# In one pair of attention tiles, Q and K change places in the seven-product scheme, and K's second half is put out last

## The chip, the cores and the metric

The kernel runs on one core of a Trainium2 chip. The metric is the device time of one execution in microseconds. Three executions of the kernel before took 2127.22, 2127.66 and 2129.57 us; the median, 2127.66 us, is the time before.

## The reference

The model is a decoder trunk of two layers over 1024 positions of width 1024. Layer 0 mixes tokens with a spatial gate, layer 1 with dilated attention; each is followed by a dense MLP. The change lies in the attention layer, which computes, cut to what matters:

```python
qkv = (h @ w_qkv).astype(float32).reshape(B, S, 3, 3, 8, 64)      # Q, K, V; 3 dilation groups; 8 heads
for g, (window, dil) in enumerate(((128, 1), (512, 4), (2048, 16))):
    # blocks of 128 queries against their own and the previous block of keys, keys gathered by stride
    s = einsum('bnqrhc,bnkrhc->bnrhqk', q, k) * 64 ** -0.5
    logits = where(valid, s + bias, -1e30)
    m = max(logits); p = exp(logits - m); den = sum(p); num = einsum('bnrhqk,bnkrhc->bnqrhc', p, v)
# the three groups' numerators and denominators are merged per head with exp(m_g - max m)
o = num_sum / den_sum
return o @ w_out
```

## The kernel before, in words

**Units.** The attention is cut into 12 units: four pairs of heads, and for each the three dilation groups in the order 1, 2, 0. A unit has three tiles of 128 columns of `w_qkv`: tile 0 is Q, tile 1 is K, tile 2 is V. A tile (i, m) is tile m of unit i. Unit 1 is group 2 of the first pair of heads, unit 2 is group 0 of the same heads.

**Pairs.** After a start by plain products, the tiles are computed two at a time, in the order of the list `quads` (L1568 to L1570). Two tiles, the two halves of the contraction and the two halves of the sequence make a 2x2 block product, done by `seven` (L1224) with seven block products in the place of eight. One block product is 12 matmuls of 128x512 on the tensor engine: four slices of the contraction, three matmuls each, because every fp32 operand is split in a high and a low part. The products come in the order 6, 1, 5, 7, 2, 3, 4. The four results are ready at different times: result (1, 1), the second tile's second half of the sequence, after product 7; (0, 0) after product 2; (0, 1) after product 3; (1, 0) after product 4. The first index is the tile's place in the pair. In the pair that the change touches, number 1 in the list, K of unit 2 had place 0 and Q of unit 2 place 1.

**Putting a result out.** `put_out` calls `out_qk` (L1190) for Q and K: an addition on the vector engine (L1205), where the result is a sum of two, then the high part on the scalar engine (L1209) and the low part on the vector engine (L1210). Where the first half of a K is put out, the tile's slots are taken, and the recording of the program first goes on with the attention until the scores of the unit before are all recorded (`flow.until(lambda: U[i - 1].scored.t is not None)`, L1195). Only the tensor engine's order is kept as it is recorded; a scheduler orders the other engines.

**Attention beside the products.** `attention` (L1351) is a generator that `flow.pump()` resumes between the products' matmuls, at times that the program estimates with fixed latencies. For each unit and each of four blocks j it issues the transposes of the probabilities (`turned`, L1313: L187 in the profile, `at<-ident,t`), the scores of the next block (`scores`, L1288: `at<-k,q`), and the products of probabilities and V (`values`, L1326: `at<-tr,V`). Behind the scores stand the vector engine's reductions (L1307) and four exponentials on the scalar engine (L1309); behind the transposes a split in high and low part (`tr`, L205 on the scalar engine, L206 on the vector engine); behind the values two copies to `N` (L1346). In the profile the products of a pair read `mm<-y,wp` or `mm<-t,wp`, by the kind of their moving operand.

**Other work around it.** Each pair's weights are loaded by the sync engine's queue (`r<-in_w_qkv`), combined on GpSimd and split on the scalar and vector engines while the pair before runs. When unit 0's values are done, its `N` is stored to memory (`away<-N`, L1391), and K of unit 2 takes the slot that this `N` held. When a unit's scores are done, its statistics go out and come back in another order (`sc<-st`, `ex<-sc`, L1432 and L1434), for the merge of the groups (L1450 on).

Of the kernel before, what the change touches and what calls it, by code (L numbers as in the profile page):

```python
# [33 lines left out]
def blk(b, n=1):  # L34
    return slice(b * P, (b + n) * P)
# [77 lines left out]
def trunk(ctx: ExitStack, tc: tile.TileContext, xT, w_u, w_v, w_o, w_s, b_s, w_qkv, w_bo, rel,  # L113
          w_up, w_dn, w_dl, vecs, onehot, outT):
    nc = tc.nc
    flow = Flow()
# [56 lines left out]
    def mm_bank():  # L173
        return psm.tile([P, HALF], F32, tag="mm", name="mm")
# [33 lines left out]
    def weight(src, place=None):  # L208
        place = place or (lambda name: wpool.tile([P, D], F32R, tag="w", name=name))
        lo, hi = place("wlo"), place("whi")  # L210
        for i in range(2):
            split(hi[:, half(i)], lo[:, half(i)], load(src[:, half(i)]))
        return hi, lo
# [215 lines left out]
    def plain(src):  # L429
        w = {}  # L430
        for j in range(2):
            for i in range(2):
                w[i, j] = wpair().split(load(src(i, j)))
        return w

    def up(layer, q):
        return lambda i, j: w_up[layer, q, i, j]
# [86 lines left out]
    def load_x(s, k):  # L524
        i = nc.sync.dma_start(h[k][:, half(s)], xT[k * P:(k + 1) * P, half(s)])
        if s:
            tc.keep_in_program_order(i)
        return i
# [100 lines left out]
    for gi, chunks in enumerate(((0, 1, 2), (3, 4, 5), (6, 7))):  # L629
        banks = {}  # L630
        for k in range(KT):
            if gi == 0:
                x = load_x(0, k)
                scaled(0, k)
            if gi == 0 or gi == 1 and k > 1:
                with tc.issue_after((gelus[5] if gi else x).ins):
                    w = weight(w_v[k])
            else:
                w = weight(w_v[k])
# [20 lines left out]
            for e, i, n, f in order:  # L660
                x, c = ys[n // 4][k], blk(n % 4)
# [30 lines left out]
    for tiles in ((0, 1, 2), (3,), (4,), (5, 6, 7)):  # L692
        w = [weight(w_u[m]) for m in tiles]
        for s in range(2):
            for i, m in enumerate(tiles):
                b = mm_bank()
# [9 lines left out]
    for tiles in ((0, 1), (2,), (3,), (4, 5, 6, 7)):  # L706
        w = [weight(w_o[m]) for m in tiles]
        for s in range(2):
            for i, m in enumerate(tiles):
                b = mm_bank()  # L710
# [3 lines left out]
            if tiles[-1] == 7:  # L714
                start_terms(sq[s], s, 1, terms)
                if s == 0:
                    first = [plain(up(0, q)) for q in range(2)]
# [324 lines left out]
    xa = Terms()  # L1042
# [45 lines left out]
    def order_of(two):  # L1088

        a, b = (U[i].g for i, _ in two)  # L1090
        return b if a == b or 0 in (a, b) else 0
# [65 lines left out]
    def out_v(i, s, a, b, go):  # L1157

        u = U[i]
        ready = []  # L1160
        with tc.high_priority(offset=PRIO):
            if u.g < 2:
                t = temp()
                if b is None:
                    put(stored(t, u.g), runs(a, u.g), None)
                elif go == u.g:
                    put(stored(t, go), stored(a, go), runs(b, go))
                elif u.g == 0:
                    put(unrolled(t, go), a.rearrange("p (r q) -> p q r", r=DIL[go]), unrolled(b, go))
                else:  # L1170
                    put(t.rearrange("p (r q) -> p q r", r=4), own(a, u.g), own(b, u.g))
                ready.append((s, t))
            else:
                for e in range(2):
                    if e not in u.vt:
                        u.vt[e] = temp()
                    c = slice(8 * e, 8 * e + 8)
                    if b is None or go == 2:
                        put(u.vt[e].rearrange("p (r q) -> p r q", r=8)[:, :, 32 * s:32 * s + 32],
                            (runs if b is None else stored)(a, 2)[:, c, :], None if b is None else runs(b, 2)[:, c, :])  # L1180
                    else:
                        put(u.vt[e].rearrange("p (r q) -> p q r", r=8)[:, 32 * s:32 * s + 32, :], own(a, 2)[:, :, c],
                            own(b, 2)[:, :, c])
                u.out += 1
                if u.out == 2:
                    ready = [(e, u.vt.pop(e)) for e in range(2)]
        for part, t in ready:
            flow.add(v_side(i, t, part), LAT["ve"] + (500 if b is None else 1500) + (5000 if i == 0 else 0))

    def out_qk(i, m, s, a, b, over, go):  # L1190

        u = U[i]
        if m not in u.tiles:
            if m == 1 and i > 0:
                flow.until(lambda: U[i - 1].scored.t is not None)  # L1195
            u.tiles[m] = [slot((P, S), F32R, f"{'qk'[m]}{e}") for e in range(2)]
        hi, lo = (runs_at(t, s, u.g) for t in u.tiles[m])
        sc = -0.125 if m == 0 else 1.0
        with tc.high_priority(offset=PRIO):
            if b is None:  # L1200
                a = stored(a, go) if over else runs(a, u.g)
            else:
                t = a if over and u.g == go else temp()
                if u.g == go:
                    nc.vector.tensor_tensor(stored(t, go), stored(a, go), runs(b, go), op=ALU.add)  # L1205
                else:
                    nc.vector.tensor_tensor(t.rearrange("p (r q) -> p q r", r=DIL[u.g]), own(a, u.g), own(b, u.g), op=ALU.add)
                a = stored(t, u.g)
            nc.scalar.activation(hi, a, AF.Copy, scale=sc)  # L1209
            nc.vector.scalar_tensor_tensor(lo, a, sc, hi.bitcast(F32), op0=ALU.mult, op1=ALU.subtract)  # L1210
        u.out_qk = getattr(u, "out_qk", 0) + 1
        if u.out_qk == 4:
            u.q, u.k = u.tiles[0], u.tiles[1]
            u.qk.t = flow.t

    def out(tile, s, a, b=None, over=False, go=0):

        i, m = tile
        if m == 2:
            out_v(i, s, a, b, go)  # L1220
        else:
            out_qk(i, m, s, a, b, over, go)

    def seven(w, x, more, put_out, begun=None, first=False, go=0):  # L1224

        def one(p, bank=None):
            new = bank is None
            bank = mm_bank() if new else bank
            product(bank, w[p], x.t[p], p in (2, 3, 4) and not (first and p == 3))
            more()  # L1230
            return bank

        def copied(src):
            t = temp()
            with tc.high_priority(offset=PRIO):
                nc.scalar.activation(stored(t, go), runs(src, go), AF.Copy)  # L1236
            return t

        def plus(x, y, out=None):
            out = temp() if out is None else out  # L1240
            with tc.high_priority(offset=PRIO):
                nc.vector.tensor_tensor(stored(out, go), stored(x, go), runs(y, go), op=ALU.add)
            return out

        if first:
            a = one(1)
            u = copied(a)
            d = one(3)
            plus(u, one(6), u)
            one(2, a)  # L1250
            put_out(0, 0, a)
            e = one(7)
            c22 = plus(u, e)
            f = one(5)
            plus(c22, f, c22)
            put_out(0, 1, plus(u, f), d, True)
        else:
            u = one(6)
            if begun:
                begun()  # L1260
            u = copied(u)
            a = one(1)
            plus(u, a, u)
            d = one(5)
            c22 = plus(u, d)
            e = one(7)
            put_out(1, 1, c22, e, True)
            one(2, a)
            put_out(0, 0, a)
            one(3, d)  # L1270
            put_out(0, 1, u, d)
        one(4, e)
        put_out(1, 0, u, e, True)
        if first:
            put_out(1, 1, c22, None, True)

    def geometry(g, j):
# [273 lines left out]
    def ahead_of_last():  # L1551

        N = [slot(name="N") for _ in range(3)]
        for hp in range(3):
            nc.sync.dma_start(N[hp], kept_N[hp])
        yield 4000
        for hp in range(3):
            for i in range(2):
                split_N(hp, i, N[hp][:, half(i)])
                yield 900  # L1560
            proj_load(hp)
            yield 900
        proj_load(3)
        for k in range(KT):
            h[k] = slot(name=f"h{k}")
            nc.sync.dma_start(h[k], hd[k])

    quads = [((1, 2), (1, 1))]  # L1568
    for i in range(2, NU, 2):
        quads += [((i, 1), (i, 0)), ((i, 2), (i + 1, 0)), ((i + 1, 1), (i + 1, 2))]  # L1570

    flow.add(attention())
    for s in range(2):
# [9 lines left out]
        if s == 0:  # L1583
            w = Weights(qkv(*quads[0]), late=FIRST, apart=True)
# [4 lines left out]
    for n, two in enumerate(quads):  # L1589
        wn = Weights(qkv(*quads[n + 1])) if n + 1 < len(quads) else None  # L1590
        more = ahead(wn)
        more()
        for i, m in two:
            if m == 1:
                U[i].bias = bias_tile(U[i].hp, U[i].g)
        seven(w, xa, more, lambda i, s, a, b=None, over=False: out(two[i], s, a, b, over, order_of(two)), None if wn else lambda: flow.add(ahead_of_last()), n == 0, order_of(two))
        w = wn
    half_done.t = flow.t

# [5 lines left out]
    first = [plain(up(1, 0))]  # L1605
# [108 lines left out]
```

## Time and profile before

| what | value |
|---|---|
| timed executions, median | 2127.66 us |
| the profiled execution: its time | 2126.29 us |
| the profiled execution: its span | 2124.6 us, so 1.7 us lie around it |
| TensorE busy | 2099.4 us (99%) |
| VectorE busy | 1585.8 us (75%) |
| ScalarE busy | 1105.1 us (52%) |
| granted TensorE clock, mean | 0.997 |

The span runs from the first to the last instruction. A row of the timeline gives the start in us from the span's start, the duration, the engine, the line, the operation with what it writes and reads, the count of merged instructions and, in brackets, the idle time before it with what ended it. Matmuls overlap their neighbours, so how long a run of them holds the engine is read from its start to the start of the next run. The attention layer's pairs begin near 970 us; pair 1 runs from about 999 to 1034 us.

### The profile page before, as it was taken

The page shows a single profiled execution, that of the slowest core. Times are in us where ns is not written, and L with a number is a line of the kernel's source. Part 1 is how long each engine was busy: PE and PEld are TensorE (multiplying, and loading weights), DVE is VectorE, ACT ScalarE, POOL GpSimd, SP SyncE. Part 2 cuts the span into 40 slices and gives each one's busy share as a digit, 9 for nine tenths or more (in the row PEclk, how much of TensorE's full clock was granted, in tenths as well). Part 3 has the DMA queues.
Part 4 walks back from the last instruction along what each step waited for, and adds up shares of the span by engine and source line. Part 5 has one row for each costly group of instructions (what it writes and reads, how often), then busy time and mean ns, then how long its engine had stood idle before and what let it go on. Part 6 is the DMA issues. An engine that isn't in the chain of part 4 may idle for free.

```text
span 2124.6 us, 30462 instructions
## 1 busy us (share of the span) xinstructions
PE 2099.4 (99%) x10426; PEld 1740.8 (82%) x10426; DVE 1585.8 (75%) x2917; ACT 1105.1 (52%) x2264; POOL 562.6 (26%) x417
## 2 busy tenths in 40 slices
PE   8999999999999999999999999999999999999998
PEld 7888887888878888888888888887888887888887
DVE  7975258576689888888675867678876667988886
ACT  7644136554574444346665656665555556544443
POOL 2100213233323223542112222202132332332245
PEclk9999999999999999999999999999999999999999
DMA  6411114455354444311212122151155544554432
GB/s 224 142 62 50 40 43 135 160 177 193 133 180 164 158 140 141 117 80 52 61 52 58 58 60 54 49 175 36 64 179 186 186 146 149 177 164 144 138 106 80
DMA packets 162415, 250.21 MB, mean 118 GB/s; under 512 B 33625, under 2 KB 51156, under 8 KB 162260
## 3 DMA queue, kind: packets, MB, share of 16 engines
q1 hardware_dynamic: 161936, 248.09, 35.9%
q8 instruction: 82, 1.34, 0.3%
q14 instruction: 73, 0.60, 0.1%
q10 hardware_dynamic: 324, 0.18, 0.0%
HBM read 181.98 MB, written 66.23 MB: 117 GB/s over the span
## 4 chain that ended last, share of the span: by engine, by line
PE 90%; DVE 5%; ACT 2%; issue 1%; DMA 1%; SPq 0%; DVEq 0%; ACTq 0%
PE at L180 44%; PE mm L180 44%; PE at L187 2%; DVE wp L206 1%; DVE t L206 1%; DVE hx L206 1%; DMA t<-hid 1%; DVE h L340 0%; DVE h L940 0%; ACT t L1309 0%; ACT wp L205 0%; DMA h<-hd 0%; DVE raws L498 0%; DVE y L206 0%; SPq L169 0%
## 5 line engine op out<-in xcount | busy, mean ns | idle before, releaser
L205 ACT ACTIVATE wp<-r 128x512 fp32r<-128x512 f32 (+3 forms) x490 | 294.7, 605 | 465.4 <-PE at L180 287.9
L180 PE MATMUL at<-hx,wp 128*128 128x512 f32 x1770 | 413.8, 389 | 5.1 <-DVE wp L206 3.2
L206 DVE TENSOR_TENSOR wp<-r,wp 128x512 fp32r<-128x512 f32 (+3 forms) x490 | 372.1, 763 | 38.6 <-ACT wp L205 34.7
L180 PE MATMUL mm<-y,wp 128*128 128x512 f32 x1608 | 398.5, 394 | 1.0 <-ACT t L1236 0.5
L180 PEld LDWEIGHTS at<-hx,wp 128*128 128x128 f32 x1770 | 331.8, 188 | 76.4 <-DVE wp L206 4.1
L180 PEld LDWEIGHTS mm<-y,wp 128*128 128x128 f32 x1608 | 299.6, 189 | 66.4 <-DVE h L340 1.6
L180 PE MATMUL at<-t,wp 128*128 128x512 f32 x1344 | 314.1, 389 | 0.2 <-DVE t L803 0.2
L180 PEld LDWEIGHTS at<-t,wp 128*128 128x128 f32 x1344 | 252.2, 188 | 53.0 <-DVE t L803 0.7
L410 POOL TENSOR_TENSOR t<-r 128x512 f32<-128x512 f32 (+3 forms) x78 | 111.4, 1428 | 680.8 <-DMA r<-in_w_dn 312.9
L412 POOL TENSOR_TENSOR r<-r 128x512 f32<-128x512 f32 (+3 forms) x77 | 115.7, 1503 | 366.6 <-DVE wp L206 333.8
L180 PE MATMUL mm<-t,wp 128*128 128x512 f32 x768 | 191.4, 396 | 0.2 <-ACT t L1153 0.2
L206 DVE TENSOR_TENSOR hx<-t,hx 128x512 fp32r<-128x512 f32 x192 | 182.0, 960 | 5.6 <-ACT hx L205 5.5
L180 PE MATMUL mm<-hx,wp 128*128 128x512 f32 x708 | 171.7, 389 | 0.1
L180 PEld LDWEIGHTS mm<-t,wp 128*128 128x128 f32 x768 | 140.6, 188 | 30.3 <-ACT t L1153 0.6
L269 POOL TENSOR_TENSOR t<-t 128x512 f32<-128x512 f32 (+1 forms) x54 | 72.2, 1337 | 347.0 <-ACT t L258 345.1
L180 PE MATMUL mm<-y,whi 128*128 128x512 f32 x512 | 158.3, 390 | 0.0
L180 PEld LDWEIGHTS mm<-hx,wp 128*128 128x128 f32 x708 | 132.7, 188 | 28.2 <-DVE b L966 0.7
L940 DVE TENSOR_TENSOR h<-h,at 128x512 f32<-128x512 f32 x144 | 97.8, 681 | 55.1 <-PE at L180 55.1
L180 PE MATMUL at<-y,wp 128*128 128x512 f32 x552 | 137.5, 390 | 0.0
L803 DVE TENSOR_TENSOR t<-t,at 128x512 f32<-128x512 f32 x116 | 79.2, 684 | 77.6 <-PE at L180 77.5
L205 ACT ACTIVATE hx<-t 128x512 fp32r<-128x512 f32 x192 | 118.4, 628 | 27.5 <-DMA t<-hid 23.0
L415 POOL TENSOR_TENSOR r<-r 128x512 f32<-128x512 f32 (+3 forms) x77 | 105.9, 1375 | 82.7 <-issue 51.4
(226 smaller groups left out, 3106.9 us busy)
## 6 DMA issues: line engine op xcount, KB each, us to landing
t<-hid SPq DMA_DIRECT2D x194, 256.0 KB, 4.9
hid<-t SPq DMA_DIRECT2D x140, 256.0 KB, 2.5
r<-in_w_up SPq DMA_DIRECT2D x128, 256.0 KB, 2.8
r<-in_w_dn SPq DMA_DIRECT2D x88, 256.0 KB, 2.7
r<-in_w_qkv SPq DMA_DIRECT2D x72, 256.0 KB, 2.6
hid<-b SPq DMA_DIRECT2D x56, 256.0 KB, 2.8
r<-in_w_v SPq DMA_DIRECT2D x48, 256.0 KB, 3.8
h<-in_xT SPq DMA_DIRECT2D x16, 256.0 KB, 3.8
```

The lines of the kernel that those rows point to most:

```text
L180: nc.tensor.matmul(out, lhsT, rhs, **kw)
L187: nc.tensor.transpose(out, src, ident)
L205: nc.scalar.activation(hi, src, AF.Copy)
L206: nc.vector.tensor_tensor(lo, src, hi.bitcast(F32), op=ALU.subtract)
L269: nc.gpsimd.tensor_tensor(self.acc, self.acc, sq, op=ALU.add)
L410: tt(r7, r[0, 0], r[1, 0], op=ALU.subtract)
L412: tt(r6, r[1, 0], r[0, 0], op=ALU.subtract)
L415: tt(r3, r[0, 1], r6, op=ALU.subtract)
L803: nc.vector.tensor_tensor(out, x, y, op=ALU.add)
L940: engine.tensor_tensor(hs[i, s], hs[i, s], src, op=ALU.add)
```

## The change

Three edits, and nothing else:

- in the list of pairs, the pair of unit 2's Q and K has Q at place 0 and K at place 1;
- for this pair (`hold`), result (1, 1), now K's second half, is only summed in place after product 7, and put out as the last of the pair, behind result (1, 0);
- so K's first half, before which the recording goes on with the attention until unit 1's scores are there, is put out after product 4 and no longer after product 2.

```diff
-    def seven(w, x, more, put_out, begun=None, first=False, go=0):
+    def seven(w, x, more, put_out, begun=None, first=False, go=0, hold=False):
...
             e = one(7)
-            put_out(1, 1, c22, e, True)
+            if hold:
+                plus(c22, e, c22)
+            else:
+                put_out(1, 1, c22, e, True)
             one(2, a)
             put_out(0, 0, a)
             one(3, d)
             put_out(0, 1, u, d)
         one(4, e)
         put_out(1, 0, u, e, True)
-        if first:
+        if first or hold:
             put_out(1, 1, c22, None, True)
...
-        quads += [((i, 1), (i, 0)), ((i, 2), (i + 1, 0)), ((i + 1, 1), (i + 1, 2))]
+        quads += [((i, 0), (i, 1)) if i == 2 else ((i, 1), (i, 0)), ((i, 2), (i + 1, 0)), ((i + 1, 1), (i + 1, 2))]
...
-        seven(w, xa, more, ..., n == 0, order_of(two))
+        seven(w, xa, more, ..., n == 0, order_of(two), n == 1)
```

Each engine executes as many instructions as before; their order differs at these places.

The tensor engine, between product 2 and product 4 of pair 1, as a difference of the two orders (`k_9124`, `k_9125`, `q_8544`, `q_8545` are the high and low parts of unit 1's K and Q, `mm<-y` x12 is product 3, the `mm<-t` rows are the first three quarters of product 4):

```order
 L180 MATMUL at<-k_9125,q_8544 128x128 x2
 L180 MATMUL at<-k_9124,q_8545 128x128 x2
+L180 MATMUL mm<-y,wp 128x512 x12
+L180 MATMUL mm<-t_8782,wp 128x512 x3
+L180 MATMUL mm<-t_8785,wp 128x512 x3
+L180 MATMUL mm<-t_8788,wp 128x512 x3
 L180 MATMUL at<-tr,V 64x128 x12
 L187 MATMUL at<-ident,t 128x128 x4
```

Before, two rounds of values, transposes and scores stood back to back between products 2 and 3; now product 3 and three quarters of product 4 (21 matmuls) stand between the two rounds.

The tensor engine where unit 2's first scores begin, inside product 1 of the next pair. Before:

```order
L180 MATMUL mm<-y,wp 128x512 x6
L180 MATMUL at<-tr,V 64x128 x12
L180 MATMUL at<-k_9479,q_9347 128x128 x2
L180 MATMUL at<-k_9480,q_9347 128x128 x2
L180 MATMUL at<-k_9479,q_9348 128x128 x2
```

Now:

```order
L180 MATMUL mm<-y,wp 128x512 x6
L180 MATMUL at<-tr,V 64x128 x12
L187 MATMUL at<-ident,t 128x128 x4
L180 MATMUL at<-k_9510,q_9417 128x128 x2
L180 MATMUL at<-k_9511,q_9417 128x128 x2
```

Unit 2's first scores keep their place behind product 6 and half of product 1; four transposes, which stood before the last quarter of product 4, now stand directly ahead of them.

The scalar engine from the first round's copies to `N` on. Before:

```order
L1346 ACTIVATE N<-at 64x256 x2
L205 ACTIVATE tr<-at 128x256
L1209 ACTIVATE k_9479<-mm 128x512
L205 ACTIVATE tr<-at 128x256
L1309 ACTIVATE t,st_9210<-t,st_9210 128x128 x4
```

Now:

```order
L1349 ACTIVATE N<-at 64x256 x2
L205 ACTIVATE tr<-at 128x256
L1209 ACTIVATE q_9417<-mm 128x512
L205 ACTIVATE tr<-at 128x256
L1209 ACTIVATE k_9510<-t 128x512
L1312 ACTIVATE t,st_9210<-t,st_9210 128x128 x4
```

The high part of a first half still stands between the two splits of the transposes (Q's in the place of K's); the high part of K's held second half now stands ahead of the exponentials of unit 1's third block, and it is the first instruction that writes the slot of unit 0's stored `N`.

More of the change, by code (lines that the diff above doesn't have):

```diff
@@ L1595, in trunk @@
                 U[i].bias = bias_tile(U[i].hp, U[i].g)
-        seven(w, xa, more, lambda i, s, a, b=None, over=False: out(two[i], s, a, b, over, order_of(two)), None if wn else lambda: flow.add(ahead_of_last()), n == 0, order_of(two))
+        seven(w, xa, more, lambda i, s, a, b=None, over=False: out(two[i], s, a, b, over, order_of(two)), None if wn else lambda: flow.add(ahead_of_last()), n == 0, order_of(two), n == 1)
         w = wn
```

## The prediction

> **What bounds the kernel now.** I read the page first, for the engine that sets the end.
>
> ```profile
> span 2124.6 us, 30462 instructions
> PE 2099.4 (99%) x10426; PEld 1740.8 (82%) x10426; DVE 1585.8 (75%) x2917; ACT 1105.1 (52%) x2264; POOL 562.6 (26%) x417
> PE 90%; DVE 5%; ACT 2%; issue 1%; DMA 1%; SPq 0%; DVEq 0%; ACTq 0%
> ```
>
> The tensor engine is busy for 99% of the span and makes 90% of the chain that ended last. So a change can only gain where this engine stands still or runs slowly, and the place to look at is the one where the change alters its order. That is the timeline of the tensor engine around product 3 of pair 1:
>
> ```profile
> 1016.74 2.90 PE L180 MATMUL mm<-y,wp 128*128 128x512 f32 x12
> 1019.48 0.88 PE L180 MATMUL at<-tr,V 128*64 128x128 f32 x12
> 1020.20 0.62 PE L187 MATMUL at<-ident,t 128*128 128x128 f32 x4
> 1020.75 0.89 PE L180 MATMUL at<-k,q 64*128 64x128 f32 x12
> 1021.63 0.27 PE L180 MATMUL at<-tr,V 128*64 128x128 f32 x1
> 1022.09 0.58 PE L180 MATMUL at<-tr,V 128*64 128x128 f32 x6 [0.18 <-DVE tr L206]
> 1022.85 0.51 PE L180 MATMUL at<-tr,V 128*64 128x128 f32 x5 [0.18 <-DVE tr L206]
> 1023.64 1.48 PE L187 MATMUL at<-ident,t 128*128 128x128 f32 x4 [0.28 <-ACT t L1309]
> 1025.06 0.88 PE L180 MATMUL at<-k,q 64*128 64x128 f32 x12
> 1025.87 4.60 PE L180 MATMUL mm<-y,wp 128*128 128x512 f32 x12
> 1030.32 2.21 PE L180 MATMUL mm<-t,wp 128*128 128x512 f32 x9
> ```
>
> The first row is product 2; then come two rounds of attention without a product between them, and product 3 at 1025.87. From start to start, the first round's values take 1020.20 - 1019.48 = 0.72 us and its four transposes 0.55; the second round's values take 1023.64 - 1021.63 = 2.01 and its transposes 1.42. Product 2 holds the engine for 2.74 us, product 3, as many matmuls of one size, for 4.45. The stretch is slow twice over. The table by windows tells the second cause:
>
> ```profile
> 1022.60:1026.00 3.40, 2.76 (x23) 1.79 (x23) 1.85 (x11) 2.87 (x12) 0.00 (x0) 1.00 0.01 2
> 1026.00:1029.40 3.40, 3.40 (x9) 2.63 (x10) 1.44 (x10) 1.73 (x9) 0.00 (x0) 0.50 0.00 0
> 1029.40:1034.00 4.60, 4.60 (x32) 3.94 (x31) 2.05 (x3) 1.97 (x4) 1.09 (x1) 1.00 0.23 13
> ```
>
> The columns are the busy times of PE, PEld, DVE, ACT and POOL, then the granted clock. Right behind 3.4 us in which the tensor engine was busy for only 2.76, its clock was granted at 0.50 for 3.4 us, and product 3 ran there. What the second round waited for stands in the timeline of the other engines:
>
> ```profile
> 1021.47 0.59 ACT L1209 ACTIVATE k<-mm 128x512 fp32r<-128x512 f32 x1
> 1021.95 0.39 ACT L205 ACTIVATE tr<-at 128x256 fp32r<-128x256 f32 x1
> 1022.37 0.42 DVE L206 TENSOR_TENSOR tr<-at,tr 128x256 fp32r<-128x256 f32 x1 [0.34 <-ACT tr L205]
> 1022.71 0.28 DVE L1307 CUSTOM_DVE_ANT_0 t<-at,b 128x128 f32<-128x128 f32 x1
> ```
>
> and, in the chain of waits in order of time:
>
> ```profile
> 1023.10 1.66 ACT t L1309 x8
> ```
>
> The values need the split of transposes that ended at 1020.75 (K's high part stands in the middle of that split), and the next transposes need four exponentials of scores that ended at 1021.63. With nothing else recorded between the rounds, this latency lies bare.
>
> **The change part by part.** *The second round moves* behind product 3 and three quarters of product 4. Its values then find their splits ready and its transposes their exponentials: in the rows above the split ends at 1022.79 and the last exponential at 1024.76, and the round will not begin before 1021.63 + 2.74 + 2.04 = 1026.4 (product 3 at product 2's pace, the nine matmuls as below). Saved: (2.01 - 0.72) + (1.42 - 0.55) = 1.29 + 0.87 = **2.16 us**. This cover is 1026.4 - 1022.8 = 3.6 us for the values, and some 1.7 us for the exponentials, wanted behind the values at 1027.1 and done near 1025.4, since K's held second half stands ahead of them with some 0.6. Without the cover, the 2.16 us stay.
>
> *The clock.* If the engine is not idle there, I take it that the clock stays at 1.00 as in the stretches around: 4.45 - 2.74 = **1.71 us**. This agrees with 3.4 us at 0.50, which costs 1.7. The bounds are 0 and 1.71; I take the upper one, because the row of windows shows the drop directly behind the only stretch here in which the engine was not fully busy. [...]
>
> *What stands at new neighbours.* These are rows from behind the nine matmuls of product 4 to the place where the two orders meet again (the last row):
>
> ```profile
> 1032.36 0.88 PE L180 MATMUL at<-tr,V 128*64 128x128 f32 x12
> 1033.08 0.62 PE L187 MATMUL at<-ident,t 128*128 128x128 f32 x4
> ...
> 1036.98 1.52 PE L180 MATMUL mm<-y,wp 128*128 128x512 f32 x6
> 1038.34 0.88 PE L180 MATMUL at<-tr,V 128*64 128x128 f32 x12
> 1039.15 0.95 PE L180 MATMUL at<-k,q 64*128 64x128 f32 x12
> 1040.04 1.67 PE L180 MATMUL mm<-y,wp 128*128 128x512 f32 x6
> 1041.55 4.27 PE L180 MATMUL mm<-t,wp 128*128 128x512 f32 x18
> ...
> 1048.81 5.61 PE L180 MATMUL mm<-y,wp 128*128 128x512 f32 x24
> ```
>
> Six matmuls take 1.36 us between a product and attention and 1.51 behind scores, so a changed neighbour is worth some 0.15 us. The number of attention stretches stays four, so I take 0.05 us of loss, within 0.2 to either side.
>
> *K's second half is held.* Nothing is added: the sum in place is the addition that stood there, and high and low part are issued as before, later. What is late next is unit 2's K: both halves now come behind product 4, where Q's first half alone came before. The price is in that half's rows:
>
> ```profile
> 1035.16 0.68 DVE L1205 TENSOR_TENSOR t<-t,mm 128x512 f32<-128x512 f32 x1
> 1035.87 0.63 ACT L1209 ACTIVATE q<-t 128x512 fp32r<-128x512 f32 x1 [0.62 <-DVE t L1205]
> 1036.54 0.69 DVE L1210 SCALAR_TENSOR_TENSOR q<-t,q 128x512 fp32r<-128x512 f32 x1
> 1013.97 0.34 SPq L1391 DMA_DIRECT2D away<-N  x1
> away<-N SPq DMA_DIRECT2D x3, 512.0 KB, 4.1
> ex<-sc SPq DMA_DIRECT2D x8, 16.0 KB, 3.2
> sc<-st SPq DMA_DIRECT2D x8, 8.0 KB, 4.0
> 1049.87 0.17 DVE L1451 TENSOR_TENSOR mn<-mn,ex 128x8 f32<-128x8 f32 x1
> ```
>
> From the sum's start to the low part's end that was 2.07 us. Product 4 should end near 1026.4 + 0.72 + 0.55 + 0.81 + 0.7 = 1029.2. Ahead of the sum stand the reductions of unit 1's last block on the vector engine, and ahead of the high part its four exponentials on the scalar engine, 1.66 us behind scores that end near 1028.5; with half a us to their start they end near 1030.7, the high part near 1031.3 and the low part near 1032.0. Unit 2's first scores come 12 + 6 matmuls, values and transposes behind product 4, 2.6 + 1.3 + 0.72 + 0.55 = 5.2 us (at 2.74 / 12 = 0.23 us a matmul rather less), near 1034.4. So about 2.4 us of cover; without it each us late is a us lost. Queued behind the held half's high part are the exponentials; it writes the slot whose store was issued at 1013.97 and, at 4.1 us, landed near 1018.1, ahead of 1022.4, where the high part comes up. Unit 1's statistics leave near 1031, go out in 4.0 us and come back in 3.2, near 1039; the merge wants them at 1049.87 less what is gained, near 1046: nothing. The temporary that holds the sum is freed near 1031 and next wanted by a split near 1035: nothing.
>
> *The sum:* 2.16 + 1.71 - 0.05 = 3.8 us. The profiled execution took 2126.29 us, its span and 1.7 around it; the span should become 2120.8 and the time 2122.5. The median of the runs, 2127.66, is 1.4 above the profiled one; I take the same 3.8 off it: **2123.9 us**. No engine but the tensor engine lies on the path behind, so I let all of it reach the end.
>
> **The rivals.** *The clock drop is chance.* [...] Then the timed executions never paid the 1.71 us: 2127.66 - 2.1 = 2125.5 us. For it: the stretches of attention around are not all fully dense either and have no drop. Against it: the timed runs are longer than the profiled one, which has the drop. [...]
>
> *More than one drop.* [...] Then the gain is 3.8 + 1.7 = 5.5 and the time 2122.2 us. Against it: the windows show no second one.
>
> *The stall moves.* The recording still waits for unit 1's scores, now before K at the pair's end; if the exponentials there or unit 2's K come late, the same 3.8 us are lost a few us on: 2127.7 us. Against it: the order shows 21 matmuls between the rounds and the cover above is 1.7 us or more everywhere.
>
> *Slower.* The held half's high part waits for the store of `N`. All exponentials of unit 1 queue behind it. It decides from a landing that uses up their cover of 1.7 us and the gain: 1022.4 + 1.7 + 3.8 = 1027.9, 13.9 us after its issue against 4.1 in the row. A landing at 1034 would cost 6.1 us more and a drop of the clock 1.7: 2127.7 + 7.8 = 2135.5 us.
>
> **How the numbers follow.** The sum 0.50, the drop as chance 0.22, a second drop 0.13, the stall moves 0.10, slower 0.05. About 0.2% (4.3 us, here 2123.4 and 2131.9) is what a measurement of this kernel tells from no change. The sum lies 0.5 us inside that bound; by scatter of about 1 us in the medians, 0.3 of its chance falls outside: 0.15, with the second drop's 0.13 and a little of the first rival 0.3 faster; 0.65 within; 0.05 slower. The range of 8 in 10 goes from the second drop to the drop as chance with 0.6 and 1.5 us of scatter: 2121.6 to 2127.0.
>
> **What would show it.** Right: between product 2 and product 4 no bracket on the tensor engine, values of 0.72 and transposes of 0.55 us in both rounds, product 3 in 2.74 us, granted clock 1.00 throughout, and the `mm<-y` x24 row at about 1045.0 in the place of 1048.81. The clock step is wrong if a window of 0.50 remains near it. The prediction is wrong if a bracket appears ahead of unit 2's first scores, naming K (L1209 or L1210), or the scalar engine sits idle ahead of K's high part until a transfer lands.

## The result

Ten executions of each kernel: before 2127.56 us in the median (2125.37 to 2129.57), the changed kernel **2122.69 us** (2121.82 to 2124.18). The two medians are 4.9 us apart. The measured ratio is 0.9983, with a 95% interval of 0.9975 to 0.9990; it is not the quotient of the medians (0.9977). By it the changed kernel takes 3.6 us less, within 2.1 to 5.3. For the experiments too, "less" and "more" are read from the ratio. The forecast was 3.8 us less, 2123.9 us.

The page of the changed kernel:

```profile
span 2120.1 us, 30458 instructions
PE 2096.5 (99%) x10426; PEld 1739.9 (82%) x10426; DVE 1585.0 (75%) x2917; ACT 1103.7 (52%) x2264; POOL 563.5 (27%) x417
PE 93%; DVE 4%; ACT 1%; issue 1%; DMA 1%; SPq 0%; DVEq 0%; ACTq 0%
```

The counts of instructions on each engine are those of before, the chain is still the tensor engine's, and DVE and ACT have each a percent less of it. The timeline of the tensor engine over the place in question, changed kernel:

```profile
1017.27 2.88 PE L180 MATMUL mm<-y,wp 128*128 128x512 f32 x12
1019.99 0.88 PE L180 MATMUL at<-tr,V 128*64 128x128 f32 x12
1020.71 0.62 PE L187 MATMUL at<-ident,t 128*128 128x128 f32 x4
1021.26 0.89 PE L180 MATMUL at<-k,q 64*128 64x128 f32 x12
1022.08 3.02 PE L180 MATMUL mm<-y,wp 128*128 128x512 f32 x12
1024.93 2.20 PE L180 MATMUL mm<-t,wp 128*128 128x512 f32 x9
1026.97 0.88 PE L180 MATMUL at<-tr,V 128*64 128x128 f32 x12
1027.69 0.62 PE L187 MATMUL at<-ident,t 128*128 128x128 f32 x4
1028.24 0.89 PE L180 MATMUL at<-k,q 64*128 64x128 f32 x12
...
1035.22 0.95 PE L180 MATMUL at<-k,q 64*128 64x128 f32 x12
...
1045.57 5.61 PE L180 MATMUL mm<-y,wp 128*128 128x512 f32 x24
```

No bracket is left. The second round's values take 1027.69 - 1026.97 = 0.72 us and its transposes 0.55, as the first round's; product 3 takes 1024.93 - 1022.08 = 2.85 us. From the first round's values to the `mm<-y` x24 row, where the two orders meet again, it is 1045.57 - 1019.99 = **25.58 us**; before it was 1048.81 - 1019.48 = **29.33**. That is 3.75 us, of the 4.5 by which the spans of the two profiled executions differ. The changed kernel came to the stretch 0.5 us later, and some 1.3 us fall behind it, in work that the change does not touch. The largest piece found there is a wait for split weights near 1800 us, 1.61 us in the execution of before and 1.04 in that of the changed kernel; this wait differs among executions of other kernels as well (1.73 us with only the exchange of places, 1.61 without any wait, 1.07 with the edits in all pairs).

A window of the changed kernel (busy PE, PEld, DVE, ACT, POOL, then the granted clock) shows a fully busy engine and a full clock where product 3 runs and the second round begins:

```profile
1023.40:1026.80 3.40, 3.40 (x17) 2.81 (x16) 2.41 (x12) 2.70 (x10) 0.00 (x0) 1.00 0.01 2
```

Unit 2's K, the thing that was to be late next, in the timeline of the other engines of the changed kernel:

```profile
1030.60 0.68 DVE L1205 TENSOR_TENSOR t<-t,mm 128x512 f32<-128x512 f32 x1
1031.65 0.62 ACT L1209 ACTIVATE k<-t 128x512 fp32r<-128x512 f32 x1
1032.30 0.69 DVE L1210 SCALAR_TENSOR_TENSOR k<-t,k 128x512 fp32r<-128x512 f32 x1 [0.41 <-ACT k L1209]
```

Its low part ends at 1032.99, 2.2 us ahead of unit 2's first scores at 1035.22.

### The profile page after: what moved, and what is told of

It is laid out like the page before. It is cut to its first block, busy times and chain, and to the rows that moved or that the text cites. A ratio compares the mean times of both kernels' runs of the same rounds, so it can differ in the third digit from the quotient of the medians.

```text
span 2120.1 us, 30458 instructions
## 1 busy us (share of the span) xinstructions
PE 2096.5 (99%) x10426; PEld 1739.9 (82%) x10426; DVE 1585.0 (75%) x2917; ACT 1103.7 (52%) x2264; POOL 563.5 (27%) x417
## 4 chain that ended last, share of the span: by engine, by line
PE 93%; DVE 4%; ACT 1%; issue 1%; DMA 1%; SPq 0%; DVEq 0%; ACTq 0%
PE at L180 45%; PE mm L180 45%; PE at L187 3%; DVE wp L206 1%; DVE h L940 0%; DVE t L206 0%; DVE h L340 0%; DMA t<-hid 0%; DVE hx L206 0%; ACT wp L205 0%; ACT t L1312 0%; DVE t L1640 0%; DMA r<-in_w_dn 0%; DMA r<-in_w_v 0%; DVE y L206 0%
```

## The experiments

The theory: two rounds of attention without a product between them lay the latency of their splits and exponentials bare (2.2 us of stalls), and the idle time lowers the tensor engine's clock behind them. The rivals: that the lowered clock is chance; that not the order gains, but Q's new place or the held half of K. Each experiment shared its chip with executions of the kernel before. The first four shared 33 of them (2125.98 us in the median, 2123.51 to 2129.13), the next four 33 others on another chip (2125.17, 2123.22 to 2128.93), the last two 21 (2125.74, 2123.72 to 2129.28).

**The changed kernel again.** No edit.

> The changed kernel once more, to stand on one chip beside the others. The theory (two rounds of attention back to back cost 2.2 us of stalls and, through them, 1.7 us of lowered clock): 3.8 us less than before, product 3 again in about 2.7 us and no window of lowered clock there. The rival that the lowered clock is chance: it may show up here, and the gain is then nearer 2.1.

Measured: 2124.11 us, ratio 0.9989 (0.9980 to 0.9998), so 2.3 us less (0.4 to 4.3). The first row of the stretch and the row where the orders meet:

```profile
1021.58 0.88 PE L180 MATMUL at<-tr,V 128*64 128x128 f32 x12
...
1047.16 3.11 PE L180 MATMUL mm<-y,wp 128*128 128x512 f32 x13
```

The stretch takes 25.58 us, to the hundredth what it took the first time. What differs between the two executions (3.1 us in their spans of 2120.1 and 2123.2) lies elsewhere in the program. (The view from which the last row is taken ends at 1050 us and so counts 13 of its 24 matmuls; the same holds for the next experiment.) The clock stays at 1.00 and product 3 takes 2.86 us, as the theory has it; the interval of the time holds both the theory's 3.8 us and the rival's 2.1.

**Only the wait is left out.**

```diff
-            if m == 1 and i > 0:
+            if m == 1 and i > 0 and i != 2:
                 flow.until(lambda: U[i - 1].scored.t is not None)
```

> Q and K keep the places they had before and nothing is held, but for unit 2's K the recording does not go on with the attention first; the tensor engine then gets the same order as in the changed kernel. The theory: only the order counts, so the same 3.8 us less than before. The rival that Q's place or the held half of K is what gains: no gain, about the time before.

Measured: 2123.22 us, ratio 0.9985 (0.9977 to 0.9994), 3.2 us less. The stretch:

```profile
1019.50 0.88 PE L180 MATMUL at<-tr,V 128*64 128x128 f32 x12
...
1045.12 5.15 PE L180 MATMUL mm<-y,wp 128*128 128x512 f32 x22
```

25.62 us. So the tensor engine's order does it; neither Q's place nor the held half is needed for it. They are one way to have K's first half put out later, and leaving out the wait for this unit is another.

**The idle time filled.** Before's order, with ten matmuls that the result does not use:

```diff
+    def filler(bank, n):
+        x = xa.t[1][0].hi
+        for _ in range(n):
+            nc.tensor.matmul(bank, x[:, 0:P], x, start=True, stop=True, skip_group_check=True)
...
             pt = at_bank()
+            if u is U[1] and j == 2:
+                filler(pt, 2 if out else 3)
...
         pv = at_bank()
+        if u is U[1] and j == 1:
+            filler(pv, 5)
```

> The kernel before with ten more matmuls of 128x512 where the tensor engine stood still: five ahead of the second round's values, three and two ahead of its transposes, written to banks that are written anew behind them. They do nothing for the result. They take 10 x 0.22 = 2.2 us, about the stalls' length. The theory (the stalls lower the clock): scores of the second round begin as late as before, no window of lowered clock, product 3 in 2.7 us, and 1.7 us less than before in all. The rival that the lowered clock is chance or has another cause: product 3 stays at 4.4 us and the time at that of before or up to 2 us above it.

Measured: 2125.57 us, ratio 0.9997 (0.9988 to 1.0006). The timeline of the tensor engine:

```profile
1021.68 1.42 PE L1316 MATMUL at<-y 128*128 128x512 f32 x5
...
1025.39 0.89 PE L180 MATMUL at<-k,q 64*128 64x128 f32 x12
1026.21 3.02 PE L180 MATMUL mm<-y,wp 128*128 128x512 f32 x12
1029.06 2.20 PE L180 MATMUL mm<-t,wp 128*128 128x512 f32 x9
```

The second round's scores begin 1025.39 - 1021.68 = 3.71 us behind the first round's end, against 1025.06 - 1021.63 = 3.43 before: the ten matmuls lie in the stalls but for 0.28 us. The clock stays at 1.00, and product 3 takes 2.85 us in the place of 4.45. So the profile came out as the theory has it, but the time did not: 0.6 us less, with an interval from 2.6 less to 1.3 more, against 1.7 expected. Either the lowered clock is not paid in every execution, or the filler does not prevent it in every one. The next experiment shows that the first happens.

**Only the held half.** K keeps place 0, so it is Q's second half that is held:

```diff
-        quads += [((i, 0), (i, 1)) if i == 2 else ((i, 1), (i, 0)), ((i, 2), (i + 1, 0)), ((i + 1, 1), (i + 1, 2))]
+        quads += [((i, 1), (i, 0)), ((i, 2), (i + 1, 0)), ((i + 1, 1), (i + 1, 2))]
```

> The second half is held to the pair's end, but Q and K keep the places they had before, so it is Q's half that is held, and K's first half is put out after product 2 as before. The tensor engine's order is that of before. The theory: the stalls and the lowered clock stay, the time is that of before within 0.5 us (the scalar engine has one instruction of 0.6 us less ahead of the first round's splits and one more behind them). The rival that holding is what gains: 2 to 4 us less.

Measured: 2126.62 us, ratio 1.0002 (0.9993 to 1.0011): no gain. Its timeline answers more than it was asked:

```profile
1024.87 0.51 PE L180 MATMUL at<-tr,V 128*64 128x128 f32 x5 [0.51 <-DVE tr L206]
1025.66 1.48 PE L187 MATMUL at<-ident,t 128*128 128x128 f32 x4 [0.28 <-ACT t L1312]
1027.07 0.88 PE L180 MATMUL at<-k,q 64*128 64x128 f32 x12
1027.88 3.02 PE L180 MATMUL mm<-y,wp 128*128 128x512 f32 x12
1030.74 2.20 PE L180 MATMUL mm<-t,wp 128*128 128x512 f32 x9
```

its windows:

```profile
1023.40:1026.80 3.40, 2.27 (x15) 1.27 (x15) 2.18 (x11) 2.84 (x12) 0.00 (x0) 1.00 0.02 6
1026.80:1030.20 3.40, 3.39 (x23) 2.81 (x24) 1.60 (x10) 2.55 (x11) 0.00 (x0) 1.00 0.00 0
```

and the two ends of the stretch:

```profile
1021.18 0.88 PE L180 MATMUL at<-tr,V 128*64 128x128 f32 x12
...
1049.24 5.61 PE L180 MATMUL mm<-y,wp 128*128 128x512 f32 x24
```

The stalls are there and are a little longer than before, with 2.27 us busy of 3.40 against 2.76; but the clock stays at 1.00, and product 3 takes 2.86 us. In this execution the same order paid the stalls and not the clock. The first rival, the drop as chance, is right in this much, and the one profile of the filled order proves nothing by itself: product 3 is as fast here without a filler.

**Before again.** The same program with four source lines more.

> The kernel before, the same program with four source lines more. It asks whether the lowered clock behind the two rounds is there in another execution. [...] The rival that the lowered clock is chance: product 3 in 2.7 us, no window at 0.50.

Measured: 2126.55 us, ratio 1.0002 (0.9993 to 1.0011). The timeline:

```profile
1024.06 1.63 PE L187 MATMUL at<-ident,t 128*128 128x128 f32 x4 [0.28 <-ACT t L1312]
1025.62 1.54 PE L180 MATMUL at<-k,q 64*128 64x128 f32 x12
1027.09 4.95 PE L180 MATMUL mm<-y,wp 128*128 128x512 f32 x12
1031.88 2.20 PE L180 MATMUL mm<-t,wp 128*128 128x512 f32 x9
```

the row where the orders meet (the stretch begins at 1019.90), and a window:

```profile
1050.37 5.63 PE L180 MATMUL mm<-y,wp 128*128 128x512 f32 x24
```

```profile
1024.80:1030.90 6.10, 6.10 (x24) 4.75 (x24) 1.69 (x10) 3.31 (x14) 0.00 (x0) 0.50 0.04 1
```

Here the clock is at 0.50 for all of this window, and by narrower windows from 1024.4 to 1031.3, for 6.8 us, from inside the second round's transposes on; the scores take 1.47 us against 0.81, and product 3 takes 4.79, more than the 4.45 of the first profile. With the first profile of before (3.4 us at 0.50) and the one with the held half (none), three executions of one tensor order show three lengths of the drop.

Their stretches price the stalls and the drop apart: 1049.24 - 1021.18 = 28.06 us in the held half, with no drop; 29.33 in the first profile of before; 1050.37 - 1019.90 = 30.47 here. One wait of the held half is 0.33 us longer than that of before (0.51 against 0.18), so an estimate for the order of before with no drop is 28.06 - 0.33 = 27.73. Against the changed kernel's 25.58 the stalls are then worth 2.15 us, the drop of 3.4 us costs 29.33 - 27.73 = 1.60, and the drop of 6.8 us costs 2.74.

**Only the exchange of places.**

```diff
-        quads += [((i, 1), (i, 0)), ((i, 2), (i + 1, 0)), ((i + 1, 1), (i + 1, 2))]
+        quads += [((i, 0), (i, 1)) if i == 2 else ((i, 1), (i, 0)), ((i, 2), (i + 1, 0)), ((i + 1, 1), (i + 1, 2))]
```

> Q and K change places but nothing is held: K's second half is put out after product 7, and the recording goes on with the attention there, one product earlier than before. Two rounds stand back to back again, ahead of product 2. The theory: the stalls of 2.2 us and the lowered clock come back there, the time is that of before within 1 us. The rival that Q's place is what gains: 2 to 4 us less.

Measured: 2129.17 us, ratio 1.0019 (1.0010 to 1.0027): 4.0 us **more**, a miss; expected was the time of before within 1 us. Its windows:

```profile
1017.70:1021.10 3.40, 2.70 (x30) 2.06 (x28) 2.75 (x5) 3.36 (x13) 0.00 (x0) 1.00 0.18 70
1021.10:1024.50 3.40, 2.44 (x17) 1.46 (x17) 1.87 (x11) 2.36 (x12) 0.00 (x0) 0.99 0.22 77
1024.50:1027.90 3.40, 3.40 (x17) 2.90 (x18) 1.69 (x10) 2.49 (x11) 0.00 (x0) 0.50 0.00 0
1027.90:1031.30 3.40, 3.40 (x10) 2.63 (x9) 0.00 (x0) 0.08 (x1) 0.00 (x0) 0.51 0.14 5
```

Ahead of product 2 the engine is slack in two windows running, (3.40 - 2.70) + (3.40 - 2.44) = 1.66 us idle against 0.64 in the window before, and the clock is low for 6.8 us (two times 3.4). The stall is of the same kind and larger, and it comes one product earlier. There the first round waits as well, for the low part of V:

```profile
1018.21 0.81 PE L180 MATMUL at<-tr,V 128*64 128x128 f32 x10 [0.17 <-DVE V L1144]
```

Its values take 1018.86 - 1017.76 = 1.10 us in the place of 0.72. None of the eleven executions of this kernel has a mean granted clock of 0.998; they show 0.995 to 0.997.

**No wait at any unit's K.**

```diff
             if m not in u.tiles:
-            if m == 1 and i > 0:
-                flow.until(lambda: U[i - 1].scored.t is not None)
                 u.tiles[m] = ...
```

> The kernel before without the recording's wait for any unit's K. The theory: no other pair shows stalls with a lowered clock, so there is little more than the 3.8 us to be had: 3 to 4.5 us less than before. A rival: the waits keep later pairs from colliding, and the time comes back to that of before or above it.

Measured: 2125.69 us, ratio 1.0002 (0.9993 to 1.0011). The theory's number was wrong and the rival held. Unit 2's place has no stall here either, but later a new one comes up. The timeline of the tensor engine, the row where the orders meet and a later pair, and then of the vector engine:

```profile
1046.19 5.63 PE L180 MATMUL mm<-y,wp 128*128 128x512 f32 x24
...
1203.62 0.22 PE L180 MATMUL at<-tr,V 128*64 128x128 f32 x1
1205.46 1.57 PE L180 MATMUL at<-tr,V 128*64 128x128 f32 x17 [1.61 <-DVE tr L206]
```

```profile
1200.86 1.78 DVE L1208 SCALAR_TENSOR_TENSOR q<-t,q 128x512 fp32r<-128x512 f32 x1
...
1204.72 1.28 DVE L206 TENSOR_TENSOR tr<-at,tr 128x512 fp32r<-128x512 f32 x2
```

The values wait for a split that stands on the vector engine behind Q's low part, here 1.78 us long, and operations of the merge. Eighteen matmuls of products stand between the transposes and these values, as many as in the kernel before, where they were enough; here the split comes too late for them. At the first row this execution is 2.6 us ahead of that of before (1048.81 - 1046.19), at its end 0.3 us behind (spans 2124.9 and 2124.6). The new wait is 1.6 of these 2.9 us; where the rest went was not followed.

**The change in every pair of one unit's Q and K.**

```diff
-        quads += [((i, 0), (i, 1)) if i == 2 else ((i, 1), (i, 0)), ...]
+        quads += [((i, 0), (i, 1)), ...]
...
-        seven(w, xa, more, ..., order_of(two), n == 1)
+        seven(w, xa, more, ..., order_of(two), two[0][0] == two[1][0] and n > 0)
```

> The change in every pair that holds one unit's Q and K. The theory: the other pairs have nothing to gain, and K's two halves come last in each; within 1 us of the changed kernel, that is 3 to 4.5 us less than before. The rival: K late in a pair costs a stall ahead of the next unit's scores, some 0.5 to 1 us for each of four pairs, and the gain shrinks to 0 to 2 us.

Measured: 2130.18 us, ratio 1.0020 (1.0011 to 1.0028), 4.3 us more than before, beyond the rival's price too. Unit 2's place is as in the changed kernel (1045.42 - 1019.84 = 25.58 us for the stretch). Its tensor engine has new waits later on:

```profile
1204.45 1.58 PE L180 MATMUL at<-tr,V 128*64 128x128 f32 x17 [1.26 <-DVE tr L206]
...
1431.83 0.97 PE L180 MATMUL at<-k,q 64*128 64x256 f32 x11 [1.84 <-DVE st L1310]
```

Not K late ahead of scores, as the rival had it, but scores behind reductions of other scores (the second row's wait names the reduction's line), and behind that wait too the clock fell:

```profile
1433.00:1436.40 3.40, 3.40 (x9) 2.64 (x9) 2.80 (x15) 3.40 (x12) 0.00 (x0) 0.50 0.05 16
```

The two rows and a third wait, 0.31 us at 1143.66, are 3.4 us of new waits, and a wait ahead of the MLP's products at 1548.83 is 1.26 us against 0.23 before; the rest of the difference was not followed. The edits were made in all pairs at once, so these runs do not tell which pair causes which wait.

**The filled order again, and the same filler where nothing stalls.**

> The ten filling matmuls in the order before, a second time, since the first interval held both theories. By the runs so far the lowered clock behind the stalls shows in some executions and not in all, so on the mean it is worth about 1 us: theory, 1 us less than before (0.5 to 1.5), product 3 in 2.7 to 2.9 us, the mean granted clock 0.998 in more of the executions than before. The rival that the stalls have nothing to do with the lowered clock: the time of before within 0.5 us and the same shares of granted clock.

Measured: 2125.41 us, ratio 0.9997 (0.9988 to 1.0006), product 3 in 2.86 us; by the interval both theories stand once more. By the granted clock the theory has the better of it: 8 of the 11 executions show 0.998, against 8 of the 21 of before on the same chip. The means of the executions are 1.0 us (here) and 0.6 us (the first filled run) below those of before.

> The same ten matmuls ahead of the same round in the changed kernel, where the engine does not stand still. Theory: here they cost their full 2.2 us, so the time is that of the other filled kernel within 0.5 us, about 1 us less than before, and the values and transposes of the second round keep 0.72 and 0.55 us. The rival that the engine had room there after all: 3 us less than before, as the changed kernel without them.

Measured: 2125.70 us, ratio 0.9997 (0.9989 to 1.0006). The filler stands in the changed kernel's second round and costs in full:

```profile
1021.00 0.88 PE L180 MATMUL at<-tr,V 128*64 128x128 f32 x12
...
1048.92 5.61 PE L180 MATMUL mm<-y,wp 128*128 128x512 f32 x24
```

The stretch takes 27.92 us, 2.34 more than the changed kernel without the filler, and the interval leaves out the rival's 3 us less. In the order before, the first filled execution took 27.88:

```profile
1019.60 0.88 PE L180 MATMUL at<-tr,V 128*64 128x128 f32 x12
...
1047.48 5.63 PE L180 MATMUL mm<-y,wp 128*128 128x512 f32 x24
```

Two orders with the same work and no idle time take the same; what the change gains, then, is idle time and the clock behind it.

**The clock over all executions.** Each execution has a mean granted clock. A drop of 3.4 us at 0.50 lowers it by 0.0008, so that its third decimal tells roughly whether there was one anywhere in the program; 0.996 speaks for more than one. (In the profiles of before and of the changed kernel the last 9.7 and 7.2 us, in which the engine has little left to do, run at a clock of 0.50; the highest mean of any execution is 0.998.) The columns are executions, those at 0.998, and the mean time of these:

```
order before (33 + 33 + 21 shared, 11 of "before again")   98   42   2124.9 us
the filled order before (11 + 11)                          22   15   2125.2 us
the changed order (11 + 11 of "only the wait")             22   15   2123.0 us
```

Among the executions at 0.998 the changed order is 1.8 us better, about the stalls alone; over all of them it is 2125.95 - 2123.47 = 2.5 us better in the mean. The share at 0.998 is 43% with the stalls and 68% with the filler or in the changed order. Several chips are mixed in this. On the chip of the first four experiments alone, 14 of the 44 executions with the stalls (33 of before, 11 of the held half) show 0.998 and 6 show 0.996; of the 33 without stalls (the changed kernel again, only the wait, the filled order) 22 show 0.998 and none 0.996. On the chip of the last two it is 8 and 6 of 21 with the stalls, and 15 and 1 of 22 in the two filled kernels. By this measure the drops are fewer where nothing stalls, with a filler as with the change. On the first of these chips the changed order is 2.7 us better in the mean, and 2.0 us among the executions at 0.998.

Beside it stand the profiles: of four with the two rounds back to back and unfilled, three show a drop behind them; of the eight others none does at this place. Chance has its part at other stalls too. Near 617 us eight of the profiles show the tensor engine idle for 1.22 to 1.62 us, and two of these (the held half and the filled changed kernel) show 3.4 us at 0.52 and 0.51 behind it.

## Why the prediction was right

*What bounds the kernel, and the place.* Right. The change acts on this stretch of the tensor engine, by 3.75 us in the profiles.

*The second round moves.* Right: 0.72 and 0.55 us, as read from the first round. The nearest rows were rows of the same shape in the same place, and little had to be guessed; by the stretch of the held half, which has no drop, the stalls are worth 2.15 us (estimated above) against the forecast's 2.16. The covers held too: the splits and exponentials were done ahead, K 2.2 us ahead (2.4 forecast), no wait for the store of `N`. One detail of K's cover was read the wrong way: at 0.23 us a matmul the eighteen matmuls take 4.1 us and not 3.9, so the cover is rather more, not less.

*The clock.* A clock that can fall behind the stalls agrees with the runs: three of four profiles with the stalls show the drop at this place and none of the eight without them, and 68% of the executions show 0.998 where the stalls are gone or filled, against 43% with them. The timed medians of the filled kernels alone do not resolve it. The size was that of one execution. The drop costs 1.60 us, by the estimate above, where it is 3.4 us long; the forecast's 1.71 compares product 3, which stands behind scores, with product 2, which does not, and the same product behind scores takes 2.85 us at full clock. And three executions of the order paid 0, 1.6 and 2.7 us. The two rivals on either side, the drop as chance and more than one drop, are both real, in different executions; the forecast took the middle one for the rule. As a mean it is too much: the filled runs are 0.6 and 1.0 us below before in the mean and pay 0.28 us for the filler by the profile, so an estimate of the mean price is 0.9 to 1.2 us, and about 3 us for the whole change. That the measured median met the forecast (2122.69 against 2123.9) is in part luck: the first ten executions showed 3.6 us less by the ratio, the eleven of the second time 2.3, those of "only the wait" 3.2. The stalls' 2.2 us were the certain part of the gain.

What decides whether a drop comes, and how long it lasts, no run shows: behind one tensor order it was 3.4 us at 0.50 in the first profile of before, 6.8 us at 0.50 in that of before again, and none in that of the held half.

*New neighbours.* 0.05 us of loss were set; the stretch less the stalls and the clock is 0.1 us from what was measured (29.33 - 2.16 - 1.71 = 25.46 against 25.58), close to the 0.11 by which the clock's term was too large (1.71 against 1.60). *The stall moves* did not come about for this change, but did for its relatives: the exchange alone has a larger stall one product earlier, and with the edits in all pairs new ones come up. *Slower* did not come about either: the held half's high part did not wait for the store of `N`.

## What to carry to other kernels

Where the bounding engine has an order of its own, look for the one place at which that order has nothing to do between a result and its use; moving ready work there gained the latency here, 2.15 us by the estimate above. Two ways of doing it, the change and the wait left out, gave the same stretch (25.58 and 25.62 us). Read the price of the stall from rows of the same kind that did not stall, but take a lowered clock behind it from several executions, not from one. An edit that gains at such a place is no rule for the places that look like it: made in all pairs, it cost 4.3 us in sum.

## What the runs showed of the hardware

In the first profile of before the granted clock fell to 0.50 behind idle pieces of 0.28 us and less that sum to 0.64 us in 3.4, and in the held half it stayed at 1.00 behind 1.13 us idle in 3.4. These sums are lower bounds: the second round's values and transposes took 2.16 us longer than the first's. The row of four transposes counts as busy for 1.48 us, while their weight loads, 0.14 us each, come one at a time, 0.38 to 0.39 us apart, as their exponentials end; the second of the four:

```profile
1024.03 0.14 PEld L187 LDWEIGHTS at<-ident,t 128*128 128x128 f32 x1 [0.25 <-ACT t L1309]
```

In both profiles of the filled order the clock stayed at 1.00 at this place, behind matmuls whose result is not used. In the variant without any wait, Q's low part took 1.78 us on the vector engine, against a median of 0.69 for this operation; the kernel before has such a long one too (1.80 us at most). What slows it was not tested.
